# Joint to the up projection: another place in the queues for a token tile's sums, the third unit's bound and scale, and the weight surveys

## The chip, the cores and the metric

The kernel runs on one core of a Trainium2 chip. The metric is device time in microseconds (us) of one execution: the median of several runs. Beside the runs one execution was profiled; its trace gives every instruction with its start and length, counted from the start of the span. The engines are TensorE (PE in the profile; PEld is its weight load), VectorE (DVE), ScalarE (ACT), GpSimd (POOL), and SyncE (SP), which here only issues transfers.

## The reference

One encoder layer over 1024 tokens of width 1024, with three residual sub-layers, each followed by a layer norm:

```python
h = layer_norm(x)
h = layer_norm(a*h + hybrid_mixer(h))          # mLSTM heads and neighbourhood attention
h = layer_norm(a*h + memory_xattn(h, mem))     # cross-attention into 256 memory tokens
h = layer_norm(a*h + conv_ffn(h))

def conv_ffn(x, ...):
    h = x @ w_up + b_up                        # 1024 -> 2 * 2816
    h = depthwise_conv(h, w_dw, width=3) + b_dw   # over positions
    g, u = split(h, 2)
    return (gelu(g) * u) @ w_down + b_down
```

The change lies at the joint between the cross-attention and the up projection of `conv_ffn`.

## The kernel before

All is one launch, written with a tile framework. The instructions are recorded in the order of the Python code, and a scheduler then orders each engine's queue by a simulated timeline (`schedule_with_timeline_sim=True`); what was recorded earlier goes first where both are ready. `tc.issue_after(x.ins)` adds an order edge: what the block records on the engine of `x` goes behind `x` in that engine's queue, and instructions on other engines are not bound by it. Each engine then works through its queue in order on the chip.

Float32 products are made of three fp16 products (`mm3`, lines 224 to 226): every operand is split into a high half `hi` (ScalarE, L203) and a low half `lo` (VectorE, L204), both scaled by a power of two.

*The end of the cross-attention.* Tokens come in eight tiles of 128, in the order `todo = [0, 2, 1, 3, 4, 6, 5, 7]`. `out_d(n)` makes the output of the n-th of them: products into bank `S`, residual (L1490), norm (`ln_tile`: statistics L237 and L239, variance plus epsilon L241, power on GpSimd L242, and for the last tile one VectorE step L244 that applies them), and the store to memory (L1493). `to_B(r, tt)` then makes the tile an operand of the up projection: eight transposes on TensorE (L1389), evictions with the norm's weights on ScalarE (L1284) and VectorE (L1286), and then, for an even tile, the split into `Bh` (L1405, L1406). The up projection is done by Strassen-Winograd: seven products for a two by two block of halves, an even and an odd tile being the two halves of the tokens. So an odd tile also makes sums with its even neighbour, `T1` (L1423), `T2` (L1424), `T3` (L1427) and `T4` (L1431), each split in two by `pair` (ScalarE L1419, VectorE or GpSimd L1420). The last two tiles, 5 and 7, are both odd, so their sums lie at the joint. `T1` and `T3` live in `TX1l`, `T2` and `T4` in `TX1h`; the fourth odd operand is `B22`.

*The up projection.* 22 units (`NFF`) of 128 gate and 128 up columns. For a unit: `load` (1 MB of weights into one of three raw buffers `two0`, `two1`, `ur`), `bound` (a sum of absolute values on ScalarE, L1531, cast on VectorE, L1532), `scale` (a small TensorE product, L182, and VectorE steps L183, L174 to L176, L1540), `sums` (S1 to S4 on GpSimd, L1554 to L1557), and the splits `split_A` and `split_S` (L203, L204). `prod` makes one of the seven products (four k steps of three matmuls, 12) into a bank `z`; `take` evicts a bank into `C` (L1717 to L1729). `post` does the convolution and the gate (L1691 to L1700). At the joint the units 0 and 1 are begun first: their two products that need only the even tiles (`A11`x`B11`, `A12`x`B21`: 48 matmuls), with `to_B` of tile 7 between them. The loop over the 22 rounds follows.

*Surveys.* The down projection needs the largest sums of `w_down`. `survey_down(i)` loads a piece of 512 KB into `sv[i % 2]` (L1735; the two buffers lie in the room of `vec0` and `vec1`, and `vec1` is also the room of tile 7's evicted tile, `spare1`) and sums it on ScalarE (L1736). There are 22 pieces. Before the change one goes with each round from 0 to 19, and pieces 21 and 20 go with rounds 0 and 10.

Of the kernel before, what the change touches and what calls it, by code (L numbers as in the profile page):

```python
# [14 lines left out]
OP = mybir.AluOpType  # L15
# [7 lines left out]
NFF = FF // 128  # L23
# [27 lines left out]
def run(gen):  # L51
    for _ in gen:
        pass
# [3 lines left out]
def encoder(ctx, tc, I, out):  # L57
# [172 lines left out]
        V.tensor_tensor(lo, src, hi.bitcast(F32), OP.subtract)  # L230


    def ln_tile(r, w_t, b_t, small, late=False, hold=None, eps=EPS, parts=1, pieces=2):
        st = small.tile([128, pieces, 6], F32, name="lnst", tag=f"lnst{pieces}", bufs=3 if pieces == 2 else 1)
        with (tc.issue_after(hold.ins) if hold is not None else nullcontext()):
            for i in range(pieces):
                V.bn_stats(st[:, i, :], r[:, i * D // pieces:(i + 1) * D // pieces])  # L237
        mv = small.tile([128, 2], F32, name="lnmv", bufs=3)
        V.bn_aggr(mv, st)  # L239
        rs = small.tile([128, 2], F32, name="lnrs", bufs=3)  # L240
        V.tensor_scalar(rs[:, 0:1], mv[:, 1:2], eps, None, op0=OP.add)  # L241
        G.tensor_tensor(rs[:, 0:1], rs[:, 0:1], mhalf[:, 0:1], OP.pow)  # L242
        if late and w_t is None:
            return V.tensor_scalar(r, r, mv[:, 0:1], rs[:, 0:1], op0=OP.subtract, op1=OP.mult)  # L244
        if late:
            for i in range(parts):
                c = slice(i * D // parts, (i + 1) * D // parts)
                V.scalar_tensor_tensor(r[:, c], r[:, c], mv[:, 0:1], w_t[:, c], op0=OP.subtract, op1=OP.mult)
                V.scalar_tensor_tensor(r[:, c], r[:, c], rs[:, 0:1], b_t[:, c], op0=OP.mult, op1=OP.add)
            return  # L250
        n = V.tensor_scalar(rs[:, 1:2], mv[:, 0:1], rs[:, 0:1], -1.0, op0=OP.mult, op1=OP.mult)  # L251
        A.activation(r, r, AF.Identity, scale=rs[:, 0:1], bias=rs[:, 1:2])  # L252
        if w_t is None:
            return n
        a = V.tensor_tensor(r, r, w_t, OP.mult)
        G.tensor_tensor(r, r, b_t, OP.add)
        return a
# [23 lines left out]
    with ExitStack() as ca:  # L281
# [842 lines left out]
        with ExitStack() as cn:  # L1124
# [4 lines left out]
            o = 0  # L1129
# [144 lines left out]
    with ExitStack() as cb_:  # L1274
# [105 lines left out]
                        "T2": (T24[:, 0], T24[:, 1]), "T4": (T24[:, 2], T24[:, 3])})  # L1380

        def to_B(r, tt):

            o = slice(tt // 2 * 128, tt // 2 * 128 + 128)
            pts = []
            for q in range(2):
                pt = tbank()
                for k in range(4):
                    T.transpose(pt[:, k, :], r[:, (4 * q + k) * 128:(4 * q + k + 1) * 128], ident)  # L1389
                pts.append(pt)  # L1390
            B1 = B1s[:, tt // 2]
            spare = lambda i: vecs.tile([128, D], F32, name=f"spare{i}", tag=f"vec{i}")
            if tt % 2:
                if tt == todo[-1]:
                    r = spare(1)
                dst = [r[:, i * 512:i * 512 + 512].rearrange("p (k t) -> p k t", k=4) for i in range(2)]
            else:
                dst = [B1[:, q] for q in range(2)]
            for q in range(2):
                for k in range(4):  # L1400
                    i = 4 * q + k
                    evict_wb(q, dst[q][:, k], pts[q][:, k], wb2, i)
            if tt % 2 == 0:
                for q in range(2):
                    A.activation(Bh[:, 0, q, :, o], B1[:, q], AF.Copy)  # L1405
                    V.tensor_tensor(Bh[:, 1, q, :, o], B1[:, q], Bh[:, 0, q, :, o], OP.subtract)  # L1406
                return
            if "T1" not in Bop:
                sum_homes()
            e12, e22 = dst  # L1410
            if tt == todo[-2]:
                yl = yp.tile([128, 4096], F32, name="ysum", tag="Yl")
            t12, t34 = ((yl[:, i * 1024:i * 1024 + 1024] if tt == todo[-2] else
                         wp.tile([128, WP], F32, name="wraw", tag="wraw", bufs=2)[:, :1024]).rearrange(
                "p (i k t) -> p i k t", i=2, k=4) for i in range(2))
            T1, T2, T3, T4 = t12[:, 0], t12[:, 1], t34[:, 0], t34[:, 1]
            def pair(n, src):
                h, l = (t[:, :, o] for t in Bop[n])
                a = A.activation(h, src, AF.Copy)  # L1419
                b = (G if n in ("B22", "T3") and tt not in todo[-2:] else V).tensor_tensor(l, src, h, OP.subtract)  # L1420
                return a, b

            V.tensor_tensor(T1, e12, B1[:, 0], OP.subtract)  # L1423
            V.tensor_tensor(T2, e22, T1, OP.subtract)  # L1424
            pair("T2", T2)
            pair("T1", T1)
            V.tensor_tensor(T3, e22, e12, OP.subtract)  # L1427
            if tt not in todo[-2:]:
                pair("B22", e22)
            ends = pair("T3", T3)  # L1430
            V.tensor_tensor(T4, B1[:, 1], T2, OP.subtract)  # L1431
            pair("T4", T4)
            if tt in todo[-2:]:
                pair("B22", e22)
            return ends
# [192 lines left out]
        def prod(ps, v, a, b, first, last):  # L1628
            (ah, al), (bh, bl) = units.got[v][a], Bop[b]
            for k in range(4):  # L1630
                mm3(ps, ah[:, k, :], al[:, k, :], bh[:, k, :], bl[:, k, :], first and k == 0, k == 3, skip=True)
# [13 lines left out]
        to_B(*rq.pop(0))  # L1645
        run(o6)
        next(o7)
        to_B(*rq.pop(0))
        next(o7)
        with tc.issue_after(stores[-1].ins):  # L1650
            units.load(2)
        run(o7)

        with rtx:

            X, Z, W = {}, {}, {}
            for v in range(2):
                X[v], Z[v] = bank("z"), bank("z")
                if rq and v == 1:
                    ends = to_B(*rq.pop(0))  # L1660
                prod(X[v], v, "A11", "B11", True, False)
                prod(Z[v], v, "A12", "B21", True, True)
                W[v] = bank("z")
            run(units.split_S(1))
            with tc.issue_after(ends[0].ins), tc.issue_after(ends[1].ins):
                units.bound(2, junk)

# [2 lines left out]
        with ExitStack() as cE:  # L1673
# [113 lines left out]
            for v in range(NFF):  # L1787
                loaded = units.load(v + 3) or loaded
                pr = units.prep(v + 2)
                next(pr, None)  # L1790
                if v > 1:
                    X[v], Z[v], W[v] = bank("z"), bank("z"), bank("z")
                    prod(X[v], v, "A11", "B11", True, False)
                if v > 1:
                    first = take(v, "m1")
                    with tc.issue_after(first.ins):
                        run(ending)
                units.scale(v + 2)
                if v > 1:
                    prod(Z[v], v, "A12", "B21", True, True)  # L1800
                    take(v, "C11")
                if v > 0:
                    prod(X[v - 1], v - 1, "A22", "T4", False, True)
                    take(v - 1, "C21")
                next(pr, None)
                prod(X[v], v, "S2", "T2", False, False)
                second = take(v, "u2")
                if v == 0:
                    take(1, "m1")
                    for i in range(2):  # L1810
                        take(i, "C11")
                if posts:
                    next(posts[0])
                if v == NFF - 2:
                    y_scale(0)
                    s1 = sy[0][1]
                    sd = scale_of(dsum, 14)[1]
                    y_pair(0, s1)
                next(pr, None)
                with tc.issue_after(second.ins):  # L1820
                    units.bound(v + 3, junk)
                prod(W[v], v, "S1", "T1", True, False)
                if v == NFF - 1:
                    w_pair(0, 0)
                    y_pair(2, s1)
                if v > 0:
                    prod(W[v - 1], v - 1, "S4", "B22", False, True)
                    take(v - 1, "C12")
                next(pr, None)
                prod(X[v], v, "S3", "T3", False, False)  # L1830
                take(v, "u3")
                take(v, "C22")
                ending = posts.pop() if posts else ()
                if v > 0:
                    posts.append(post(v - 1))
                if v < NFF - 2:
                    survey_down(v)
                    if v in (0, 10):
                        survey_down(NFF - 1 - v // 10)

            v = NFF - 1
            run(ending)
# [173 lines left out]
```

## Time and profile before

| | us |
|---|---|
| median of 3 runs | 1478.93 |
| lowest and highest | 1476.84, 1479.02 |
| the profiled execution | 1474.43 |
| its span, first to last instruction | 1472.4 |
| granted TensorE clock, mean | 0.993 |
| busy: DVE, ACT, POOL | 1027.0, 822.2, 559.4 |
| rounds of the up projection in the trace | about 835 to 1235 |

A row of the timeline gives the start, the length, the engine, the line, the operation, and output and inputs by the program's names. The bracket at its end is the idle time of the engine before it and what ended that. In a row of waits stand the waiting engine and line, what it waited for, and the total, the number and the longest of these waits. In a row of windows each engine's busy time is followed by its number of instructions.

### The profile page before, as it was taken

The page shows a single profiled execution, that of the slowest core. Times are in us where ns is not written, and L with a number is a line of the kernel's source. Part 1 is how long each engine was busy: PE and PEld are TensorE (multiplying, and loading weights), DVE is VectorE, ACT ScalarE, POOL GpSimd, SP SyncE. Part 2 cuts the span into 40 slices and gives each one's busy share as a digit, 9 for nine tenths or more (in the row PEclk, how much of TensorE's full clock was granted, in tenths as well). Part 3 has the DMA queues.
Part 4 walks back from the last instruction along what each step waited for, and adds up shares of the span by engine and source line. Part 5 has one row for each costly group of instructions (what it writes and reads, how often), then busy time and mean ns, then how long its engine had stood idle before and what let it go on. Part 6 is the DMA issues. An engine that isn't in the chain of part 4 may idle for free.

```text
span 1472.4 us, 21481 instructions
## 1 busy us (share of the span) xinstructions
PE 1432.3 (97%) x7996; PEld 844.1 (57%) x7996; DVE 1027.0 (70%) x1950; ACT 822.2 (56%) x1385; POOL 559.4 (38%) x440
## 2 busy tenths in 40 slices
PE   8999899999999999999999899999999999999998
PEld 6998777456766777774444444444444444444445
DVE  7867866535767778589657768887887879627333
ACT  5765465565554577424455678887777767411010
POOL 4452356502233766055114144554444400302352
PEclk9999999999999999999999999999999999999999
DMA  8845654214554643743343323333323228621111
GB/s 302 316 185 193 185 195 156 84 50 128 159 138 152 218 142 135 265 150 72 86 100 114 133 100 128 145 118 126 115 114 142 102 95 286 230 85 47 57 57 58
DMA packets 116382, 208.60 MB, mean 142 GB/s; under 512 B 40627, under 2 KB 69555, under 8 KB 112950
## 3 DMA queue, kind: packets, MB, share of 16 engines
q1 hardware_dynamic: 115984, 206.47, 42.1%
q8 instruction: 63, 1.03, 0.3%
q0 software_dynamic: 144, 0.49, 0.2%
q14 instruction: 41, 0.34, 0.1%
q10 hardware_dynamic: 150, 0.27, 0.0%
HBM read 154.15 MB, written 45.15 MB: 135 GB/s over the span
## 4 chain that ended last, share of the span: by engine, by line
PE 77%; DVE 9%; DMA 5%; ACT 4%; issue 2%; POOL 1%; SPq 0%; DVEq 0%; ACTq 0%; POOLq 0%
PE z L224 7%; PE z L226 7%; PE z L225 7%; PE dn L224 5%; PE dn L226 5%; PE dn L225 5%; PE S L224 4%; PE S L225 4%; PE S L226 4%; DVE wlo L204 2%; PE cl L224 2%; PE cl L225 2%; PE cl L226 2%; PE cu L226 1%; PE tk L225 1%
## 5 line engine op out<-in xcount | busy, mean ns | idle before, releaser
L225 PE MATMUL dn<-wlo,yp 128*128 128x512 f16 (+1 forms) x284 | 105.1, 370 | 0.0
L224 PE MATMUL dn<-whi,yp 128*128 128x512 f16 (+1 forms) x284 | 104.9, 370 | 0.0
L226 PE MATMUL dn<-whi,yp 128*128 128x512 f16 (+1 forms) x284 | 104.3, 370 | 0.0
L1692 DVE SCALAR_TENSOR_TENSOR cbuf<-C,wdw,cbuf 128x1024 f32<-128x1024 f32 x44 | 66.2, 1506 | 34.0 <-ACT cbuf L1691 34.0
L224 PEld LDWEIGHTS <-whi 128*128 128x128 f16 x540 | 52.8, 98 | 57.7 <-issue 4.6
L226 PEld LDWEIGHTS <-wlo 128*128 128x128 f16 x540 | 52.8, 98 | 57.1 <-DVE wlo L204 1.8
L225 PEld LDWEIGHTS <-whi 128*128 128x128 f16 x540 | 52.8, 98 | 54.8 <-issue 2.2
L242 POOL TENSOR_TENSOR lnrs<-lnrs,mhalf 128x1 f32<-128x1 f32 x32 | 24.0, 750 | 157.1 <-DVE lnrs L241 151.3
L1554 POOL TENSOR_TENSOR wraw<-two 128x512 f32<-128x512 f32 x15 | 31.1, 2071 | 126.7 <-issue 126.7
L204 DVE SCALAR_TENSOR_TENSOR wlo<-wraw,us,whi 128x1024 f16<-128x1024 f32 (+1 forms) x48 | 61.5, 1300 | 20.0 <-ACT whi L203 20.0
L1693 DVE SCALAR_TENSOR_TENSOR cbuf<-C,wdw,cbuf 128x1024 f32<-128x1024 f32 x44 | 71.8, 1632 | 1.1
L1691 ACT ACTIVATE cbuf<-C,bdw,wdw 128x1024 f32<-128x1024 f32 x44 | 54.5, 1238 | 21.0 <-DVE C L1729 20.3
L203 ACT ACTIVATE whi<-wraw,us 128x1024 f16<-128x1024 f32 (+1 forms) x48 | 51.1, 1103 | 16.5 <-DVE us L176 15.9
L224 PEld LDWEIGHTS <-yp 128*128 128x128 f16 x370 | 36.2, 98 | 39.9
L225 PEld LDWEIGHTS <-yp 128*128 128x128 f16 x370 | 36.2, 98 | 39.8
L226 PEld LDWEIGHTS <-yp 128*128 128x128 f16 x370 | 36.2, 98 | 39.7
L252 ACT ACTIVATE r<-r,lnrs 128x1024 f32<-128x1024 f32 x11 | 13.6, 1236 | 79.0 <-DVE lnrs L251 78.9
L224 PE MATMUL tk<-whi,Bo 128*128 128x256 f16 (+1 forms) x192 | 52.6, 274 | 2.6 <-DVE stage L204 2.6
L225 PE MATMUL tk<-wlo,Be 128*128 128x256 f16 (+1 forms) x192 | 52.4, 274 | 0.9 <-DVE wlo L204 0.9
L224 PE MATMUL tk<-whi,Be 128*128 128x256 f16 (+1 forms) x192 | 52.6, 274 | 0.4 <-DVE stage L204 0.4
L226 PE MATMUL tk<-whi,Bo 128*128 128x256 f16 (+1 forms) x192 | 52.5, 274 | 0.0
L225 PE MATMUL tk<-wlo,Bo 128*128 128x256 f16 (+1 forms) x192 | 52.5, 274 | 0.0
(556 smaller groups left out, 4839.1 us busy)
## 6 DMA issues: line engine op xcount, KB each, us to landing
two<-in_w_up_dram SPq DMA_DIRECT2D x15, 1024.0 KB
sv<-in_w_down_dram SPq DMA_DIRECT2D x22, 512.0 KB
y<-cbuf SPq DMA_DIRECT2D x22, 512.0 KB
wraw<-in_w_down_dram SPq DMA_DIRECT2D x22, 512.0 KB
ur<-in_w_up_dram SPq DMA_DIRECT2D x7, 1024.0 KB
two<-y SPq DMA_DIRECT2D x7, 1024.0 KB
r<-h SPq DMA_DIRECT2D x11, 512.0 KB
wraw<-in_w_tok_dram SPq DMA_DIRECT2D x10, 512.0 KB
```

The source lines that it names most:

```text
L203: A.activation(hi, src, AF.Copy, scale=s)
L204: return V.scalar_tensor_tensor(lo, src, s, hi, op0=OP.mult, op1=OP.subtract)
L224: T.matmul(ps, lh, rh, start=first, stop=False, skip_group_check=skip)
L225: T.matmul(ps, lh, rl, start=False, stop=False, skip_group_check=skip)
L226: return T.matmul(ps, ll, rh, start=False, stop=last, skip_group_check=skip)
L242: G.tensor_tensor(rs[:, 0:1], rs[:, 0:1], mhalf[:, 0:1], OP.pow)
L252: A.activation(r, r, AF.Identity, scale=rs[:, 0:1], bias=rs[:, 1:2])
L1554: G.tensor_tensor(S1, A21, A22, OP.add)
L1691: A.activation(c, C[:, 1:SEQ + 1], AF.Identity, scale=wdw[:, 1, j:j + 1], bias=bdw[:, j:j + 1])
L1692: V.scalar_tensor_tensor(c, C[:, 0:SEQ], wdw[:, 0, j:j + 1], c, op0=OP.mult, op1=OP.add)
L1693: V.scalar_tensor_tensor(c, C[:, 2:SEQ + 2], wdw[:, 2, j:j + 1], c, op0=OP.mult, op1=OP.add)
```

## The change

- `to_B` is cut in two: `to_B1` (transposes, evictions, and the split of an even tile) and `to_B2` (the sums of an odd tile). For tile 5, the last but one, `to_B1` keeps its place, while `to_B2` is recorded after the whole of the last `out_d`, behind an order edge to the last norm's L241 (`eased`) on VectorE.
- `pair("T4")` instead of `pair("T3")` gives the instructions `ends` that later edges refer to.
- `bound` of unit 2 is recorded right behind tile 5's sums (behind their `T4` halves on ScalarE and VectorE), no longer behind tile 7's sums and unit 1's split.
- `scale` of unit 2 is recorded behind tile 7's `to_B`, its VectorE steps behind the low half of `T4`, and no longer in round 0.
- The rounds 0 and 1 have no survey. Rounds 2 to 19 have their own piece as before, and the pieces 0, 1, 20 and 21 go as a second one with the rounds 4, 8, 12 and 16.

```diff
+    eased = [None]
 ...
-        V.tensor_scalar(rs[:, 0:1], mv[:, 1:2], eps, None, op0=OP.add)
+        eased[0] = V.tensor_scalar(rs[:, 0:1], mv[:, 1:2], eps, None, op0=OP.add)
 ...
         def to_B(r, tt):
+            t = to_B1(r, tt)
+            return to_B2(t, tt) if t else None
+
+        def to_B1(r, tt):
 ...
                 return
+            return dst
+
+        def to_B2(dst, tt):
+
+            o = slice(tt // 2 * 128, tt // 2 * 128 + 128)
+            B1 = B1s[:, tt // 2]
 ...
-            ends = pair("T3", T3)
+            pair("T3", T3)
             V.tensor_tensor(T4, B1[:, 1], T2, OP.subtract)
-            pair("T4", T4)
+            ends = pair("T4", T4)
 ...
         run(o6)
         next(o7)
-        to_B(*rq.pop(0))
+        tt = rq[0][1]
+        t = to_B1(*rq.pop(0))
         next(o7)
         with tc.issue_after(stores[-1].ins):
             units.load(2)
         run(o7)
+        with tc.issue_after(eased[0].ins):
+            ends = to_B2(t, tt)
+        with tc.issue_after(ends[0].ins), tc.issue_after(ends[1].ins):
+            units.bound(2, junk)
 ...
                 if rq and v == 1:
                     ends = to_B(*rq.pop(0))
+                    with tc.issue_after(ends[1].ins):
+                        units.scale(2)
                 prod(X[v], v, "A11", "B11", True, False)
                 prod(Z[v], v, "A12", "B21", True, True)
                 W[v] = bank("z")
             run(units.split_S(1))
-            with tc.issue_after(ends[0].ins), tc.issue_after(ends[1].ins):
-                units.bound(2, junk)
 ...
-                units.scale(v + 2)
+                if v > 0:
+                    units.scale(v + 2)
 ...
-                if v < NFF - 2:
+                if 1 < v < NFF - 2:
                     survey_down(v)
-                    if v in (0, 10):
-                        survey_down(NFF - 1 - v // 10)
+                    if v % 4 == 0:
+                        survey_down((0, 1, NFF - 2, NFF - 1)[v // 4 - 1])
```

## The prediction

> **What bounds the kernel now.** I read the page first, then the waits of TensorE, then windows of the stretch that the change touches, then each engine's timeline there. In the page TensorE is busy for nearly all of the span, so time can come only from what it still loses.
>
> ```profile
> PE 1432.3 (97%) x7996; PEld 844.1 (57%) x7996; DVE 1027.0 (70%) x1950; ACT 822.2 (56%) x1385; POOL 559.4 (38%) x440
> ```
>
> The table of TensorE's waits over the whole run (total us, times, longest) has the joint as its largest entry, and two more of its entries:
>
> ```profile
> PE z L224 <- ACT TX1l L1419: 3.7, 1, 3.7
> ...
> PE z L224 <- ACT unitYl L203: 2.2, 1, 2.2
> ...
> PE z L224 <- ACT C L1721: 1.3, 2, 1.1
> ```
>
> The windows (length, then busy us of PE, PEld, DVE, ACT, POOL, granted clock, DMA share, GB/s) show where: holes at 830 to 840 and 850 to 860, a slower clock (0.83) between them, and later rounds without any hole.
>
> ```profile
> 830.00:840.00 10.00, 5.95 (x31) 3.04 (x30) 5.92 (x11) 5.38 (x13) 1.90 (x13) 1.00 0.17 61
> 840.00:850.00 10.00, 9.58 (x38) 3.98 (x38) 5.45 (x12) 4.13 (x7) 5.63 (x4) 0.83 0.32 104
> 850.00:860.00 10.00, 6.65 (x31) 2.75 (x29) 4.93 (x5) 9.29 (x10) 3.49 (x3) 1.00 0.36 130
> ...
> 980.00:1020.00 40.00, 40.00 (x189) 18.17 (x187) 32.68 (x42) 32.53 (x39) 15.80 (x8) 1.00 0.34 123
> ```
>
> TensorE's timeline, each row with its start, its length and the idle time before it in brackets:
>
> ```profile
> 834.32 1.04 PE L1389 MATMUL tp<-ident,r 128*128 128x128 f32 x8
> 839.07 0.38 PE L224 MATMUL z<-TX1l,unitYh 128*128 128x512 f16 x1 [3.71 <-ACT TX1l L1419]
> ...
> 840.10 0.38 PE L224 MATMUL z<-TX1h,unitYh 128*128 128x512 f16 x1 [0.45 <-ACT TX1h L1419]
> ...
> 841.17 0.59 PE L225 MATMUL z<-TX1l,unitYh 128*128 128x512 f16 x1 [0.32 <-DVE TX1l L1420]
> ...
> 843.97 0.38 PE L226 MATMUL z<-TX1l,unitYh 128*128 128x512 f16 x1
> ...
> 854.42 0.39 PE L224 MATMUL z<-TX1l,unitYl 128*128 128x512 f16 x1 [2.25 <-ACT unitYl L203]
> ...
> 856.13 0.38 PE L224 MATMUL z<-TX1l,unitYh 128*128 128x512 f16 x1 [1.10 <-ACT C L1721]
> ```
>
> The prize: a first stall of 3.71 us ahead of the first product on the sums T, a stutter of 0.45 + 0.32 = 0.77 us, a slow clock (from 841.17 to 843.97 seven matmuls took 2.80 us; at the 40.00/189 = 0.212 us of the window at 980 they take 1.48, so 1.3 us lost), and a second stall of 2.25 + 1.10 = 3.35 us. Together 9.1 us, 0.6% of the run. The PE work itself is unchanged, and as the later rounds have PE at 40.00 of 40.00, what is won here should reach the end.
>
> **Edit 1: tile 5's sums behind the last norm (`eased`).** VectorE and GpSimd now, in the order of the first stall:
>
> ```profile
> 824.02 0.69 DVE L1423 TENSOR_TENSOR ysum<-r,Bf 128x512 f32<-128x512 f32 x1 [0.95 <-ACT r L1284]
> 824.63 0.74 DVE L1490 SCALAR_TENSOR_TENSOR r<-r,sc,S 128x512 f32<-128x512 f32 x1
> ...
> 829.00 0.69 DVE L1431 TENSOR_TENSOR ysum<-Bf,ysum 128x512 f32<-128x512 f32 x1
> 829.60 0.21 DVE L241 TENSOR_SCALAR lnrs<-lnmv,sc 128x1 f32<-128x1 f32 x1
> ...
> 831.45 0.86 DVE L244 TENSOR_SCALAR r<-r,lnmv,lnrs 128x1024 f32<-128x1024 f32 x1 [0.45 <-POOL lnrs L242]
> ...
> 836.50 0.69 DVE L1423 TENSOR_TENSOR wraw<-spare,Bf 128x512 f32<-128x512 f32 x1 [3.59 <-ACT spare L1284]
> ```
>
> ```profile
> 816.38 0.55 POOL L242 TENSOR_TENSOR lnrs<-lnrs,mhalf 128x1 f32<-128x1 f32 x1 [10.08 <-DVE lnrs L241]
> 829.88 1.53 POOL L242 TENSOR_TENSOR lnrs<-lnrs,mhalf 128x1 f32<-128x1 f32 x1 [12.96 <-DVE lnrs L241]
> ```
>
> Between 824.02 and 829.60 six of tile 5's sums (L1423, L1424, L1427, L1431 and two of L1420) stand ahead of the last tile's L241, 0.60 us each (829.00 to 829.60). Behind L241 they give it 6 x 0.60 = 3.6 us. The last norm's r is then done at 832.31 - 3.6 = 828.7 instead of 831.45 + 0.86 = 832.31. GpSimd's power between them took 0.55 or 1.53 us in these rows: r could be 0.98 earlier, or later by the two sums that may now slip in ahead of L244 (1.2). I keep 828.7, the row that had sums running beside it.
>
> [...]
>
> The last tile's transposes (L1389) start at 834.32 now, 2.0 us after r: they queue behind the 48 matmuls of the first four products. Their place in PE's queue is set when the program is built, and no row shows the new one: not moved, 834.32; at best at r, 828.7. I take it that they move with r, to 830.7. The first product on the sums follows the transposes by 839.07 - 834.32 = 4.75 us, so 835.45, when PE's other work ends at 834.32 + 1.04 = 835.36: 0.1 us of stall instead of 3.71.
>
> Where the six go: VectorE's idle 3.59 us ahead of 836.50 is just their 3.6, so the cover is used up and the last tile's own sums come straight behind. Between none and all six (3.6 us) delay them; I take two, 1.2 us.
>
> **Edit 2: unit 2's bound directly behind tile 5's sums.** ScalarE now:
>
> ```profile
> 834.96 2.20 ACT L1284 ACTIVATE spare<-tp,wb 128x128 f32<-128x128 f32 x6 [4.62 <-PE tp L1389]
> ...
> 840.43 1.94 ACT L1531 ACTIVATE junk<-ur 128x2048 bf16<-128x2048 f32 x1
> 842.23 0.23 ACT L1531 ACTIVATION_READ_ACCUMULATOR junk<-ur 128x1 f32 x1
> ...
> 845.57 1.06 ACT L1736 ACTIVATE sv<-sv 128x1024 f32<-128x1024 f32 x1 [2.60 <-DMA sv<-in_w_down_dram]
> ...
> 850.71 1.06 ACT L1736 ACTIVATE sv<-sv 128x1024 f32<-128x1024 f32 x1 [3.99 <-DMA sv<-in_w_down_dram]
> ...
> 851.77 1.56 ACT L203 ACTIVATE unitYl<-ur,us 128x1536 f16<-128x1536 f32 x1
> ...
> 855.32 0.76 ACT L1721 ACTIVATE C<-z,bup,us 128x512 f32<-128x512 f32 x1
> ```
>
> The bound (2.0 us from 840.43 to the end of its read at 842.46) leaves the place at 840.43 and comes behind T4's first half of tile 5. That is L241's new time, 826.0, plus its own 0.2, six sums (3.6) and L244 (0.86): 830.7, and another 0.6 for T4 itself: 831.3. The last tile's eight evictions (L1284) are then due at 830.7 + 0.64 (834.96 - 834.32) = 831.3. So the bound falls on them: between 0 (it stands behind them) and 2.0 us; ScalarE's 4.62 idle us covered it only while the transposes were late. I take half, 1.0. The cast that it feeds waits on VectorE for the same time. The first stall left: 0.1 + 1.2 + 1.0 = 2.3, saved 3.71 - 2.3 = 1.4 us. The stutter is VectorE's pace of 0.60 a step against a matmul's 0.212; I count half of it saved, 0.4. The slow clock followed an idle of 3.71, and none followed that of 2.25 (850 to 860 has 1.00): 1.3 saved.
>
> [...]
>
> **Edit 3: unit 2's scale behind the last tile's T4, no surveys before round two.** ScalarE sat 2.60 + 3.99 us for two surveys' DMAs while unit 2's split (851.77) stood behind them. Its scale, on VectorE behind a matmul (L182) that waits for the cast, and GpSimd's sums of the unit:
>
> ```profile
> 843.01 1.58 DVE L1420 TENSOR_TENSOR TX1h<-wraw,TX1h 128x512 f16<-128x512 f32 x1
> 847.68 0.29 DVE L183 TENSOR_REDUCE us<-mx 128x1 f32<-128x128 f32 x1 [3.09 <-PE mx L182]
> ...
> 848.45 0.20 DVE L1540 TENSOR_SCALAR us<-us,sc 128x1 f32<-128x1 f32 x1
> ```
>
> ```profile
> 847.42 0.22 PE L182 MATMUL mx<-identb,am 128*128 128x128 bf16 x1
> ```
>
> ```profile
> 842.46 1.59 POOL L1554 TENSOR_TENSOR wraw<-ur 128x512 f32<-128x512 f32 x1 [6.90 <-issue]
> ```
>
> The scale was ready at 848.65, 3.1 us before the split began. With the change the scale (0.97 us, 847.68 to 848.65) stands behind T4's second half, which ends at 843.01 + 1.58 = 844.59 now and 1.4 earlier then: 843.2, scale at 844.2. The split and the eviction behind it (851.77 to 856.08, 4.3 us) end at 848.5. PE, from its first product at 837.7, has 48 matmuls at 0.212 and 0.4 of stutter ahead: 848.3. About 0.2 to 0.4 of 3.35 stay; saved 3.0. Ends: nothing, or all 3.35. Late next are GpSimd's sums (842.46), which start once the last tile's buffers are free and shift with them. Behind the scale's small VectorE steps only B22's half is queued; its matmul (0.22) stands in PE's queue, and placed ahead of the T products it would hold them until the cast, up to the bound's 2.0 again, which (b) prices.
>
> The surveys are 22 before and after. Three leave the joint, and rounds 4, 8, 12 and 16 have two each. One such pair exists now, one buffer for both:
>
> ```profile
> 985.16 7.44 SPq L1735 DMA_DIRECT2D sv<-in_w_down_dram  x2
> ```
>
> ```profile
> 996.09 1.06 ACT L1736 ACTIVATE sv<-sv 128x1024 f32<-128x1024 f32 x1 [1.71 <-DMA sv<-in_w_down_dram]
> 997.05 0.19 ACT L1736 ACTIVATION_READ_ACCUMULATOR sv<-sv 128x1 f32 x1
> ```
>
> ```profile
> 884.00:902.00 18.00, 17.93 (x85) 8.06 (x83) 16.63 (x19) 15.67 (x19) 10.09 (x5) 1.00 0.36 140
> ...
> 992.00:1010.00 18.00, 18.00 (x86) 8.17 (x85) 14.63 (x17) 14.34 (x19) 7.45 (x5) 1.00 0.41 147
> ```
>
> Its price on ScalarE is 1.15 of work (996.09 to 997.24) and 1.71 of wait, 2.9, in a round with 18.00 - 14.34 = 3.7 to spare; PE lost nothing there. In the SP queue the second transfer waits for the first's reader (7.44 us for the pair), and the next store and load come later anyway. I take 0; upper end 0.6 for round 4, which has only 18.00 - 15.67 = 2.3 to spare, or 2.9 a round if a pair sits on the path.
>
> **The sum.** 1.4 + 0.4 + 1.3 + 3.0 = 6.1 us. The profiled execution (1474.43 with 1472.4 of span) would come to 1468.3. It lies 4.5 under the median of the runs shown, so I subtract from that: 1478.93 - 6.1 = 1472.8.
>
> **Rivals.** (a) The first stall stays: the queue order puts the transposes where they were, the bound and T4 only trade places. For it: 2.0 us already lie between r and transposes. Only the second stall goes, 3.0 to 3.35: 1475.8. (b) The bound takes the place of the sums: full 2.0 us ahead of the evictions and the sums move nothing, first stall 5.7. 3.0 - 2.0 = 1.0 won: 1477.9. Against it: all its data had landed (ScalarE waits for no `ur`). (c) VectorE becomes the bound: at 884 it is busy 16.63 of 18.00, and its 3.59 and 3.09 idle us in the joint vanish; its conv steps then make PE wait until the old place is reached again, and 5 of 6.1 are given back: 1477.8. Against it: 1.4 us to spare a round. (d) Slower: the four survey pairs lie on ScalarE's path at 2.9 each, 11.6 - 6.1 = 5.5: 1484.4; it decides from the third such round on, as two cost 5.8. Against it: the pair now costs PE nothing.
>
> **How the numbers follow.** Forecast 0.57, (a) 0.13, (b) 0.09, (c) 0.12, (d) 0.09. 0.2%, 3.0 us, is about what a measurement of this kernel can tell from no change. Faster: the forecast and two thirds of (a), which lies at that bound, 0.66; same 0.25: the rest of (a), (b), (c); slower (d), 0.09. All terms at their best, 9.1, give 1469.8, and the runs shown (1476.84 to 1479.02) spread by about a microsecond to either side: the range reaches from 1468.5 to 1479.5, over (a), (b) and (c), leaving (d) and a little below out. The forecast's own range is 1469 to 1475.
>
> **What would show it.** L241 of the last tile at about 826 and its L244 ending near 828.7; transposes near 830.7; no slow clock at 840 to 850; the first T product by 838; unit 2's split by 845; no wait for `sv` before round two, and 1 to 2 us each in the rounds with pairs, with PE full there. Wrong if the transposes keep their place, if the bound stands ahead of the evictions with more than its 2.0, or if PE shows new waits for C in the first rounds.

## The result, and the profile after

The changed kernel takes 1470.72 us (median of 6 runs, 1469.54 to 1473.99) against 1477.5 for the kernel before (6 runs): ratio 0.9956, 95% interval 0.9944 to 0.9969. That is 6.8 us less (4.6 to 8.3); forecast were 6.1 and 1472.8. Line numbers of the joint have moved: L241 is now L243, L244 is L246, the transposes L1395, the last tile's evictions L1286, `pair` L1431 and L1432, the bound L1543, the surveys L1752.

TensorE's waits in the whole run after the change (total us, times, longest): the two entries of the second stall are gone, and the first stall is 2.3 instead of 3.7.

```profile
PE z L224 <- ACT TX1l L1431: 2.3, 1, 2.3
...
PE z L224 <- ACT TX1h L1431: 0.4, 1, 0.4
...
PE mx L182 <- ACT spare L1286: 0.2, 1, 0.2
PE z L225 <- DVE TX1l L1432: 0.2, 1, 0.2
```

The windows of the joint after the change: 850 to 860 is full, 840 to 850 is not, and its clock is 0.83 as before.

```profile
830.00:840.00 10.00, 8.14 (x42) 4.12 (x41) 7.43 (x14) 7.53 (x15) 0.76 (x13) 1.00 0.18 64
840.00:850.00 10.00, 8.67 (x32) 3.45 (x32) 8.37 (x15) 5.52 (x8) 5.85 (x4) 0.83 0.00 0
850.00:860.00 10.00, 10.00 (x49) 4.56 (x47) 6.66 (x10) 8.09 (x10) 6.51 (x5) 1.00 0.43 157
```

Two traces are best compared from a common event. I take the first product on the even tiles (`z<-Bh`) as zero and call times from there "joint time". The end mark is the first matmul of the down projection (`dn`), which stands among the last products of the 22 rounds. First the rows of the kernel before, then those of the changed one:

```profile
823.96 0.38 PE L224 MATMUL z<-Bh,unitYh 128*128 128x512 f16 x1
...
1218.54 0.38 PE L224 MATMUL dn<-whi,yp 128*128 128x512 f16 x1
```

```profile
826.52 0.38 PE L224 MATMUL z<-Bh,unitYh 128*128 128x512 f16 x1
...
835.80 1.04 PE L1395 MATMUL tp<-ident,r 128*128 128x128 f32 x8
...
838.14 0.22 PE L182 MATMUL mx<-identb,am 128*128 128x128 bf16 x1 [0.22 <-ACT spare L1286]
840.69 0.38 PE L224 MATMUL z<-TX1l,unitYh 128*128 128x512 f16 x1 [2.33 <-ACT TX1l L1431]
...
841.73 0.44 PE L224 MATMUL z<-TX1h,unitYh 128*128 128x512 f16 x1 [0.45 <-ACT TX1h L1431]
...
842.79 0.59 PE L225 MATMUL z<-TX1l,unitYh 128*128 128x512 f16 x1 [0.20 <-DVE TX1l L1432]
...
1215.76 0.38 PE L224 MATMUL dn<-whi,yp 128*128 128x512 f16 x1
```

From zero to `dn` it was 1218.54 - 823.96 = 394.6 us and is 1215.76 - 826.52 = 389.2: the change is worth 5.3 us between these marks, in one profiled execution of each. The spans differ by only 1472.4 - 1469.6 = 2.8, because the changed kernel reached the joint 2.6 us later, though the order of TensorE's queue up to there is the same. The likely cause is the clock: ahead of the joint the trace before has four stretches of 3.41 us at half rate (a granted clock of 0.50) and that of the changed kernel six, three of them in these two windows (at 162.7, 555.2 and 589.3). Changed:

```profile
150.00:200.00 50.00, 46.15 (x383) 38.02 (x383) 37.87 (x89) 27.38 (x44) 18.33 (x28) 0.97 0.65 199
...
550.00:600.00 50.00, 46.91 (x293) 35.65 (x293) 39.18 (x115) 35.21 (x98) 27.32 (x23) 0.93 0.45 150
```

and before:

```profile
150.00:200.00 50.00, 46.56 (x398) 38.79 (x398) 36.81 (x87) 27.18 (x44) 18.35 (x28) 1.00 0.65 197
...
550.00:600.00 50.00, 45.93 (x297) 34.17 (x298) 39.06 (x124) 36.93 (x104) 26.95 (x23) 1.00 0.45 153
```

So one profile of each would have told less than half of the difference of the medians; the joint time tells 5.3, inside the interval of the medians. The remaining 1.5 us are not located; when the changed kernel was measured again, the medians differed by 5.8 us (below).

VectorE, GpSimd and ScalarE in the joint after the change:

```profile
828.99 0.21 DVE L243 TENSOR_SCALAR lnrs<-lnmv,sc 128x1 f32<-128x1 f32 x1
...
830.92 0.81 DVE L246 TENSOR_SCALAR r<-r,lnmv,lnrs 128x1024 f32<-128x1024 f32 x1
...
838.12 0.69 DVE L1435 TENSOR_TENSOR wraw<-spare,Bf 128x512 f32<-128x512 f32 x1 [1.23 <-ACT spare L1286]
```

```profile
829.28 0.93 POOL L244 TENSOR_TENSOR lnrs<-lnrs,mhalf 128x1 f32<-128x1 f32 x1 [9.80 <-DVE lnrs L243]
```

```profile
834.71 1.89 ACT L1543 ACTIVATE junk<-ur 128x2048 bf16<-128x2048 f32 x1
...
836.61 2.18 ACT L1286 ACTIVATE spare<-tp,wb 128x128 f32<-128x128 f32 x6
838.66 1.47 ACT L1733 ACTIVATE C<-z,bup,us 128x512 f32<-128x512 f32 x2
839.98 0.66 ACT L1431 ACTIVATE TX1l<-wraw 128x512 f16<-128x512 f32 x1
...
845.95 1.58 ACT L203 ACTIVATE unitYl<-ur,us 128x1536 f16<-128x1536 f32 x1 [3.15 <-DVE us L176]
```

The last norm's r is ready at 830.92 + 0.81 = 831.73, joint time 5.2 instead of 8.35. But the transposes start at 835.80, 4.1 us behind it. From them to the first T product ScalarE's queue sets the pace: T1 is ready on VectorE at 838.12 + 0.69 = 838.81, but two evictions into `C` stand ahead of its `pair`, which starts at 839.98. Unit 2's split now waits for its scale and for nothing else.

### The profile page after: what moved, and what is told of

Same layout as the page of the kernel before. It is cut to its first block, busy times and chain, and to the rows that moved or that the text cites. A ratio compares the mean times of both kernels' runs of the same rounds, so it can differ in the third digit from the quotient of the medians.

```text
span 1469.6 us, 21479 instructions
## 1 busy us (share of the span) xinstructions
PE 1435.0 (98%) x7996; PEld 847.4 (58%) x7996; DVE 1031.0 (70%) x1950; ACT 821.9 (56%) x1385; POOL 559.5 (38%) x440
## 4 chain that ended last, share of the span: by engine, by line
PE 78%; DVE 7%; DMA 5%; ACT 4%; issue 3%; POOL 2%; SPq 1%; DVEq 0%; ACTq 0%; POOLq 0%
PE z L226 7%; PE z L225 7%; PE z L224 7%; PE dn L224 5%; PE dn L226 5%; PE dn L225 5%; PE S L224 4%; PE S L225 4%; PE S L226 4%; PE tk L225 2%; PE tk L224 2%; PE tk L226 2%; PE cl L224 2%; PE cl L225 2%; PE cl L226 2%
## 5 line engine op out<-in xcount | busy, mean ns | idle before, releaser
L1708 DVE SCALAR_TENSOR_TENSOR cbuf<-C,wdw,cbuf 128x1024 f32<-128x1024 f32 x44 | 64.9, 1477 | 39.3 <-ACT cbuf L1707 39.3
L244 POOL TENSOR_TENSOR lnrs<-lnrs,mhalf 128x1 f32<-128x1 f32 x32 | 23.4, 731 | 154.9 <-DVE lnrs L243 148.1
```

What stands on the lines that cost most here:

```text
L1708: V.scalar_tensor_tensor(c, C[:, 0:SEQ], wdw[:, 0, j:j + 1], c, op0=OP.mult, op1=OP.add)
```

## The experiments

All were timed in five rounds against the kernel before on the same chip. "To `dn`" is the joint time of the first down matmul in the profiled execution.

| kernel | median us | ratio to before, 95% | to `dn` | first T product at | first stall | second stall |
|---|---|---|---|---|---|---|
| before | 1477 | 1 | 394.6 | 15.1 | 3.71 | 3.35 |
| changed, again | 1471.25 | 0.9961 (0.9949 to 0.9973) | 389.4 | 14.2 | 2.55 | 0 |
| surveys alone | 1473.37 | 0.9974 (0.9964 to 0.9984) | 391.8 | 15.1 | 3.71 | 0.34 |
| sums alone | 1475.61 | 0.999 (0.9979 to 1.0001) | 395.2 | 14.0 | 2.63 | 3.70 |
| bound and scale alone | 1471.42 | 0.9957 (0.9944 to 0.9971) | 391.2 | 15.1 | 3.50 | 0 |
| changed, surveys back | 1470.62 | 0.9965 (0.9952 to 0.9978) | 389.6 | 14.2 | 2.56 | 0 |
| changed, sums back | 1471.2 | 0.9959 (0.9946 to 0.9972) | 390.9 | 15.1 | 3.50 | 0 |
| early transposes | 1467.99 | 0.9941 (0.9928 to 0.9954) | 387.0 | 12.9 | 1.06 | 0 |
| filled stall | 1469.83 | 0.9953 (0.9939 to 0.9968) | 389.2 | 14.8 | 1.47 | 0 |
| no second surveys | 1471.01 | 0.9963 (0.9951 to 0.9976) | 389.2 | 14.2 | 2.55 | 0 |

Where a kernel has it, the first stall includes the wait ahead of the scale's small matmul (L182).

**Changed, again.** The changed kernel once more, as the distance for the others.

> The changed kernel itself, beside the other three on one chip. All theories: ratio to before 0.9944 to 0.997 as measured; it gives the distance of the other three from it.

Its two stalls (2.55 and 0) and its 389.4 us to `dn` agree with the first execution's. At joint time 89.9 it differs: here TensorE waits 0.84 us for an eviction into `C`, there it does not.

**Surveys alone.** The kernel before with the new survey rounds:

```diff
-                if v < NFF - 2:
+                if 1 < v < NFF - 2:
                     survey_down(v)
-                    if v in (0, 10):
-                        survey_down(NFF - 1 - v // 10)
+                    if v % 4 == 0:
+                        survey_down((0, 1, NFF - 2, NFF - 1)[v // 4 - 1])
```

> The kernel before with the new places of the surveys alone. Theory A (the parts add up: the second stall was the surveys' wait on ScalarE, the first stall was the sums ahead of the last norm and the place of the transposes): the first stall stays at 3.7 us, unit 2's split starts at its scale, some 3.1 us earlier, and the second stall of 3.35 falls to 0 to 0.4; 3.0 to 3.4 us faster than before, ratio about 0.998. Theory B (the surveys are the whole of the gain): as fast as the changed kernel, 5 to 7 us, ratio about 0.9955. Theory C (VectorE gives the gain back in the rounds behind): the second stall goes and the time stays within 1 us of before.

TensorE's two stalls and unit 2's split in its timeline:

```profile
840.44 0.59 PE L224 MATMUL z<-TX1l,unitYh 128*128 128x512 f16 x1 [3.71 <-ACT TX1l L1419]
...
853.60 0.38 PE L224 MATMUL z<-TX1l,unitYh 128*128 128x512 f16 x1 [0.34 <-ACT C L1721]
```

```profile
849.22 1.58 ACT L203 ACTIVATE unitYl<-ur,us 128x1536 f16<-128x1536 f32 x1 [4.86 <-DVE us L176]
```

The split starts at its scale (joint time 23.9 instead of 27.8), the second stall is 0.34 instead of 3.35, the first is untouched. Theory A; B and C fall: the time is 3.7 us lower, 2.8 by the joint time, and not the whole gain.

**Sums alone.** The kernel before with `to_B` cut in two as in the change, and tile 5's `to_B2` behind the last norm:

```diff
-        to_B(*rq.pop(0))
+        tt = rq[0][1]
+        t = to_B1(*rq.pop(0))
 ...
         run(o7)
+        with tc.issue_after(eased[0].ins):
+            ends = to_B2(t, tt)
```

> The kernel before with tile 5's sums behind the last norm alone; bound, scale and surveys as before. Theory A: L241 some 3 us earlier, the first T product 1 to 2 us earlier (no bound ahead of the last tile's evictions), the second stall stays at 2.5 to 3.4 us because the surveys' transfers still stand ahead of unit 2's split; 1 to 2 us faster, ratio about 0.999. Theory B: no difference (within 0.5 us). Theory C: no difference either, but with the first stall shorter in the trace.

```profile
840.61 0.38 PE L224 MATMUL z<-TX1l,unitYh 128*128 128x512 f16 x1 [2.63 <-ACT TX1l L1431]
...
855.95 0.39 PE L224 MATMUL z<-TX1l,unitYl 128*128 128x512 f16 x1 [2.60 <-ACT unitYl L203]
```

The first T product comes 1.1 us earlier, and the second stall is 2.60 + 1.10: what is won ahead of it waits there. The time is 1.4 us lower with an interval that touches 1, and to `dn` it is even 0.6 us longer, since this execution had two half-rate stretches at the joint (at 841.2 and 858.3, with matmuls 0.43 us apart instead of 0.22) where that of before had one (at 840.4, clock 0.50). Theory A by the trace, not shown by the time.

**Changed, surveys back.** The changed kernel with the old survey lines.

> The changed kernel with the surveys back in their old places. Theory A: unit 2's split waits on ScalarE for two survey transfers again, the second stall returns with 2.5 to 3.5 us; 1 to 3 us faster than before, ratio about 0.9985. Theory B: no faster than before. Theory C: as fast as the changed kernel, since the stall only moves.

```profile
846.38 1.06 ACT L1752 ACTIVATE sv<-sv 128x1024 f32<-128x1024 f32 x1 [4.33 <-DMA sv<-in_w_down_dram]
...
847.44 1.56 ACT L203 ACTIVATE unitYl<-ur,us 128x1536 f16<-128x1536 f32 x1
...
851.29 1.06 ACT L1752 ACTIVATE sv<-sv 128x1024 f32<-128x1024 f32 x1 [0.21 <-DMA sv<-in_w_down_dram]
```

All three theories missed a part. The surveys are back and ScalarE waits 4.33 us for one, but the second stall is not: with the earlier scale the split stands between the two surveys, no longer behind both, and is in time. My theory A had taken the surveys for the one cause. Theory C has the time right, but no stall moved: the second one is gone.

**Bound and scale alone.** The kernel before with the bound and the scale of unit 2 moved, the sums and surveys not:

```diff
-        to_B(*rq.pop(0))
+        ends = to_B(*rq.pop(0))
 ...
+        with tc.issue_after(ends[0].ins), tc.issue_after(ends[1].ins):
+            units.bound(2, junk)
 ...
                     ends = to_B(*rq.pop(0))
+                    with tc.issue_after(ends[1].ins):
+                        units.scale(2)
 ...
-            with tc.issue_after(ends[0].ins), tc.issue_after(ends[1].ins):
-                units.bound(2, junk)
 ...
-                units.scale(v + 2)
+                if v > 0:
+                    units.scale(v + 2)
```

> The kernel before with unit 2's bound and scale in their new places alone; tile 5's sums and the surveys as before. Theory A2 (the second stall needs two things at once, a late scale and a survey's transfer ahead of the split; taking away either is enough): no second stall although the surveys are back, one survey wait of some 4 us on ScalarE that nobody on the path waits for; the first stall at 3.3 to 3.7; some 3 to 4 us faster than before, ratio 0.997 to 0.998. Theory A1 (the survey's transfers alone make the second stall): it stays at 2.5 to 3.4, and the time within 1 us of before.

```profile
846.55 1.06 ACT L1749 ACTIVATE sv<-sv 128x1024 f32<-128x1024 f32 x1 [4.31 <-DMA sv<-in_w_down_dram]
...
847.61 1.56 ACT L203 ACTIVATE unitYl<-ur,us 128x1536 f16<-128x1536 f32 x1
```

Theory A2. The second stall needed a late scale and surveys ahead of the split; either edit alone takes it away (2.8 and 3.4 us to `dn`), and the second of them adds 0.9 us or less. Bound and scale were moved together, so which of the two it takes is not shown. By the medians this version is already as fast as the whole change (1471.42 against 1471.25 and 1470.72); that the sums add something shows only in the times to `dn`.

**Changed, sums back.** The changed kernel with tile 5's whole `to_B` in its old place.

> The changed kernel with tile 5's sums back ahead of the last norm (bound, scale and surveys as changed). Theory A: the first stall is 3.3 to 3.9 us again and the second stays away; 3.5 to 5 us faster than before, ratio about 0.997. Theory B: as fast as the changed kernel. Clock: if the half-rate stretch comes with any stall above 2.3 us, it shows here behind the first stall too.

```profile
839.78 0.22 PE L182 MATMUL mx<-identb,am 128*128 128x128 bf16 x1 [1.16 <-ACT spare L1286]
...
842.34 0.59 PE L224 MATMUL z<-TX1l,unitYh 128*128 128x512 f16 x1 [2.34 <-ACT TX1l L1431]
```

The stall is 1.16 + 2.34 = 3.50 again, the second stays away, and to `dn` it takes 1.5 us longer than the changed kernel: the sums' move is worth about 1 us of stall. A part of the 1.5 us is the clock: behind the first stall lies a half-rate stretch of 6.83 us here (granted clock 0.51 and 0.50 in the windows from 841.7 to 848.5), where the changed kernel has 3.41. The medians (1471.2 against 1470.72) can't tell that.

**Early transposes.** The prediction let the transposes move with r, and they did not. Here an order edge puts them between the A11 and the A12 products of the first two units (`tps[0]` is the tile's last transpose):

```diff
             for v in range(2):
-                X[v], Z[v] = bank("z"), bank("z")
-                if rq and v == 1:
-                    ends = to_B(*rq.pop(0))
-                    with tc.issue_after(ends[1].ins):
-                        units.scale(2)
+                X[v], Z[v], W[v] = bank("z"), bank("z"), bank("z")
                 prod(X[v], v, "A11", "B11", True, False)
-                prod(Z[v], v, "A12", "B21", True, True)
-                W[v] = bank("z")
+            ends = to_B(*rq.pop(0))
+            with tc.issue_after(ends[1].ins):
+                units.scale(2)
+            with tc.issue_after(tps[0].ins):
+                for v in range(2):
+                    prod(Z[v], v, "A12", "B21", True, True)
```

> The changed kernel with the last tile's transposes put between the two A11 products and the two A12 products of the first units in TensorE's queue (an order edge holds the A12 products behind them); nothing else is moved by hand. Theory A (the place of the transposes sets the first T product, 4.75 to 4.9 us behind them): transposes some 5.3 us behind the first up product instead of 9.3, the first T product at 10 to 12 us instead of 14.2, when TensorE has work until 11.4; first stall 0 to 0.7 instead of 2.3, no half-rate stretch there; 2 to 3.5 us faster than the changed kernel, ratio to before about 0.9935 to 0.995. Theory E (VectorE, with both tiles' sums, sets it): the first T product stays within 0.5 us of 14.2, and the time with it. Theory F: r is not ready when the transposes' turn comes, TensorE waits there instead, and no time is won.

```profile
830.53 1.06 PE L1397 MATMUL tp<-ident,r 128*128 128x128 f32 x8
...
837.17 0.23 PE L182 MATMUL mx<-identb,am 128*128 128x128 bf16 x1 [0.39 <-DVE am L1546]
838.06 0.38 PE L224 MATMUL z<-TX1l,unitYh 128*128 128x512 f16 x1 [0.67 <-ACT TX1l L1433]
```

```profile
831.56 2.19 ACT L1286 ACTIVATE spare<-tp,wb 128x128 f32<-128x128 f32 x6
834.13 1.93 ACT L1545 ACTIVATE junk<-ur 128x2048 bf16<-128x2048 f32 x1
...
836.03 1.47 ACT L1735 ACTIVATE C<-z,bup,us 128x512 f32<-128x512 f32 x2
837.35 0.66 ACT L1433 ACTIVATE TX1l<-wraw 128x512 f16<-128x512 f32 x1
```

The transposes start at joint time 5.35, just behind r (5.2), and TensorE loses nothing there: F falls. The first T product comes at 12.9, stall 0.67 + 0.39, no half-rate stretch follows (granted clock 1.00 from 835.9 to 850), and the time is 3.3 us below the changed kernel's on the same chip (2.4 to `dn`). Theory A in sign and size, but not in its law: the product is 7.5 us behind the transposes, not 4.8, so they set it no longer. Now the bound, which this order put behind the evictions, and two evictions into `C` stand ahead of `pair` in ScalarE's queue (837.35), and VectorE has both tiles' sums in a row, as theory E says for the rest. This version beats the kernel before, and by all signs the changed one: the two intervals just overlap, but five of its six runs lie below every run of the changed kernel (lowest 1469.54).

**Filled stall.** Eight matmuls without use ahead of the first T product:

```diff
+            pd = bank("mx")
+            (dh, dl), (eh, el) = units.got[0]["A11"], Bop["B11"]
+            for k in range(8):
+                T.matmul(pd, dh[:, k % 4, :], eh[:, k % 4, :], start=k == 0, stop=k == 7, skip_group_check=True)
```

> The changed kernel with 8 matmuls of 128x512 added in TensorE's queue between the last Z product and the first T product, whose output nobody reads; they fill most of the first stall of 2.3 us. Theory A (the half rate comes from TensorE's low activity in one stretch of 3.41 us): no half-rate stretch at the joint, the T products run at 0.216 us from the start, the first T product itself is not earlier; 1.0 to 1.4 us faster than the changed kernel. Theory G (the slow T products are slow for another reason, their operands' pace): matmuls as slow as before, no time won.

```profile
836.71 1.90 PE L1686 MATMUL mx<-Bh,unitYh 128*128 128x512 f16 x8 [1.25 <-DVE spare L1288]
```

They waited 1.25 us for a bank and pushed the first T product back by 0.65 us, to 14.8. Windows of 3.4 us around them, the first with the stall and most of the fill, the second where the half rate had been:

```profile
835.50:838.92 3.42, 2.21 (x11) 1.03 (x12) 3.38 (x7) 3.42 (x8) 0.00 (x0) 1.00 0.04 5
838.92:842.33 3.41, 2.99 (x15) 1.28 (x14) 3.41 (x7) 0.99 (x2) 1.15 (x1) 1.00 0.00 0
```

The half rate is gone: the granted clock is 1.00 in both windows, with TensorE busy for 2.21 of 3.42 us in the first, where the changed kernel has 0.77 of 3.40 and then 0.50. In this execution theory A has the cause. The price is not as theory A had it: to `dn` this kernel is as long as the changed one, and its median, 1.4 us lower, is within the intervals. The trace shows where the gain goes, a wait for ScalarE in a later round:

```profile
911.77 0.38 PE L224 MATMUL z<-Bh,unitA 128*128 128x512 f16 x1
913.36 0.38 PE L224 MATMUL z<-TX1l,unitYh 128*128 128x512 f16 x1 [1.21 <-ACT C L1741]
```

TensorE comes to the matmul at 911.77 in joint time 88.1, in the changed kernel's first execution 89.4, and then waits 1.21 us; the next product starts in joint time 89.7 here and 89.8 there. What is won ahead of that product counts only as far as ScalarE's eviction comes earlier too, as with the early transposes, where the product starts at 87.5.

**No second surveys.** The two lines `if v % 4 == 0` and its survey left out, so four pieces of `w_down` are not in the scale.

> The changed kernel without the four second surveys of the rounds 4, 8, 12 and 16 (four pieces of w_down are left out of the scale). Theory A (they are hidden): as fast as the changed kernel within 0.5 us, TensorE's waits in the rounds unchanged. Theory H (each pair costs what ScalarE waits for it): faster by up to 2.9 us for each pair that lies on the path.

1471.01 against 1471.25 us on the same chip, 389.2 against 389.4 to `dn`: the pairs are hidden, H falls.

## Why the prediction was right, point by point

The time and its sign were right, and so was the largest term. Three steps failed: the transposes did not move with r, the delays that were counted behind them did not come, and the slow clock stayed. The first two cancelled, so that the first stall came out near its forecast; that is luck. The trace shows 5.3 us where 6.1 were forecast, and the medians show 6.8, of which 1.5 are not located: that the total came out so close is in part luck too.

*L241 and r.* Forecast 3.6 us earlier; in joint time 2.5 instead of 5.6, so 3.2, and r 3.1 earlier. Right. GpSimd's power took 0.93 us, between the 1.53 and 0.55 that the working weighed, and three sums (829.12 to 830.92) slipped in ahead of L246, which started 1.93 us behind L243 (1.85 before) and 0.71 behind the end of the power (830.21): the price of the power was not what held r.

*The transposes move with r.* This step failed. They moved by 1.1 us, from 10.4 to 9.3, 4.1 us behind r: their place in TensorE's queue, set when the program was built, is now behind 43 of the 48 matmuls on the even tiles instead of behind all. The law that the first T product follows by 4.75 us held (840.69 - 835.80 = 4.89; with sums alone 4.75).

*Two of the displaced sums (1.2) and half the bound (1.0) delay the last tile.* Neither did: VectorE waited 1.23 us for the evictions, not they for it, and the bound, though it does stand ahead of the evictions, ended only 0.2 us behind the time at which they would have begun (834.71 + 1.89 = 836.60 against 835.80 + 0.64 = 836.44), so that the evictions began at 836.61 and the law's 4.75 became 4.89, 0.14 more. So the stall left, 2.3 by forecast, is 2.33 and 0.22 by other parts: late transposes in place of VectorE and ScalarE.

*The stutter.* 0.45 + 0.20 instead of 0.77; 0.1 saved, not 0.4.

*The slow clock.* This step failed too: forecast gone (1.3), measured unchanged. I had read it from the length of the stall, between 2.25 and 3.71 us; a stall of 2.33 has it (granted clock 0.50 from 841.9 to 845.3).

*The second stall.* Forecast 3.0 of 3.35, measured all of it. Right in size; the working named both the surveys and the scale as what goes, and the runs show that either is enough.

*The survey pairs.* Forecast 0, measured 0 (no second surveys): rival (d) falls. Rival (b) falls: the bound ahead of the evictions cost 0.14 us, not 2.0. Rival (c) falls in size, with 389.2 to `dn`, but the wait for `C` that it names is there: 0.84 us in the second execution of the changed kernel, 1.21 in the filled stall. (a) was half true: the transposes moved by 1.1 us only, but the first stall shrank all the same.

The sum from the trace: 3.71 - 2.55 = 1.2 and 0.1 and 3.35, 4.6 us at the joint, and 0.4 in the first rounds (waits of TensorE in the windows from 884 to 938: before 0.7, after 0.25): 5.1 of the 5.3 to `dn`.

## What to carry to other kernels

An instruction moved earlier on one engine is worth only as much as the next one in the chain moves in its own queue (r came 3.1 us earlier here, the transposes 1.1): look up how long a consumer starts behind its operand, and put an order edge there too. When a stall has two causes in a row, removing either can end it (the second stall of 3.35 us fell to 0.34 by one edit and to 0 by the other), and undoing each part of a change alone tells which of them is needed. What is won at one place can be lost at the next wait for another engine (1.21 us for ScalarE in the filled stall), so follow a gain to the end mark. Compare traces from a common event just ahead of the change, since what differs before it (2.6 us here) can be as large as the effect.

## What the hardware showed that I had not expected

TensorE's half rate, a granted clock of 0.50, did not follow from the length of one stall. In the trace before none came behind the 2.25 us of the second stall, and one came at 488.8 us, where the longest idle time in the 3.41 us ahead was 1.13 us (at 487.29, L1243). In these two traces it came in stretches of 3.41 us (or two of them) that lie on a grid: up to the joint they start at 28.0, 488.8 and 840.4 us in the trace before and at 29.5, 162.7, 490.3, 555.2, 589.3 and 841.9 in that after, each a whole number of 3.413 us behind the first of its trace (the last of each 238). The windows of 3.4 us on that grid, before (the first two around the first stall, the third in the second stall):

```profile
837.00:840.40 3.40, 0.89 (x4) 0.37 (x4) 3.36 (x7) 3.40 (x7) 0.00 (x0) 1.00 0.02 2
840.40:843.80 3.40, 3.08 (x9) 0.97 (x8) 3.38 (x7) 2.58 (x4) 1.34 (x1) 0.50 0.30 89
...
850.65:854.06 3.41, 1.52 (x8) 0.49 (x5) 0.70 (x1) 3.35 (x4) 0.00 (x0) 1.00 0.00 0
```

and after the change:

```profile
838.50:841.90 3.40, 0.77 (x3) 0.29 (x3) 3.36 (x7) 3.40 (x7) 0.00 (x0) 1.00 0.01 2
841.90:845.30 3.40, 3.20 (x8) 0.99 (x7) 3.40 (x7) 0.90 (x2) 1.23 (x1) 0.50 0.00 0
```

Where TensorE was busy for 0.77 or 0.89 of a grid window, the next one ran at 0.50; after 1.52 of 3.41, in the second stall of before, it did not, nor after 2.21 of 3.42 in the filled stall. At the joint the half rate followed the first stall in all nine executions in which that stall was 2.55 us or more (by a clock of 0.50 or 0.51 in three of them, in the other six by matmuls 0.43 us apart instead of 0.22), and in neither of the other two (clock 1.00). But busy time alone does not sort the windows: elsewhere in the trace before, 1.71 of 3.41 was followed by the half rate.

```profile
485.42:488.83 3.41, 1.71 (x10) 1.04 (x8) 3.38 (x5) 2.44 (x8) 3.41 (x2) 1.00 0.31 81
488.83:492.25 3.42, 2.44 (x11) 2.44 (x12) 3.06 (x12) 1.08 (x3) 2.21 (x3) 0.50 1.06 295
```

So these runs show no threshold, and what decides in the windows between is open. Nor did the same code always get the same clock: over the executions of the kernel before, the mean granted clock went from 0.988 to 0.994. And the trace after has a stretch at 162.7 us, long before the joint, where that before has a clock of 1.00 from 150 to 200.
